# A mixture-of-experts layer pair: slots lent and freed by other rules, scatter ordered behind gate/up, a hint on a jump; and one attention layer without GpSimd arithmetic

## The chip, the cores and the metric

The kernel runs on one core of one Trainium2 chip. The core has five engines with instruction queues of their own: TensorE (PE, matrix products, with its weight loads shown as PEld), VectorE (DVE), ScalarE (ACT), GpSimd (POOL) and SyncE (SP, which here only issues transfers). Transfers between the chip's memory (HBM) and the on-chip memory (SBUF) run on 16 DMA engines. The metric is the time of one execution in microseconds (us), lower is better.

## The reference

Two stacks of two layers each run on 256 tokens of width 1024. The first stack has causal attention with rotary positions, a gated feed-forward layer, an RWKV layer and a second feed-forward layer. The second has differential attention, attention to a memory and a mixture of experts (MoE), then sparse latent attention, attention to the memory and a second MoE. The change touches the first attention layer and both MoE layers:

```python
def moba_attention(x, w_qkv, w_o, cos, sin):
    q, k, v = jnp.split(x @ w_qkv, 3, axis=-1)
    q = apply_rope(to_heads(q), cos, sin)       # 16 heads of 64
    k = apply_rope(to_heads(k), cos, sin)
    ...
    p = jax.nn.softmax(s_all, axis=-1)          # causal scores
    ...
    return out @ w_o

def hierarchical_moe(x, w_group, b_group, w_expert, b_expert, w_gate, w_up, w_down):
    ...
    top_w = jax.nn.softmax(top_val, axis=-1) * g_gate      # 2 of 16 experts for each token
    combine = jnp.sum(jax.nn.one_hot(expert_id, N_EXPERTS) * top_w[..., None], axis=1)
    y = jnp.zeros_like(t)
    for e in range(N_EXPERTS):
        hid = jax.nn.silu(t @ w_gate[e]) * (t @ w_up[e])   # width 512
        y = y + combine[:, e:e + 1] * (hid @ w_down[e])
    return y
```

Each MoE layer is followed by `layer_norm(alpha * h + moe(h))`. All is in float32, and 16 experts with three matrices of 2 MB each have to be read for each MoE layer.

## The kernel before

**The program.** One straight line of code; a scheduler puts each engine's instructions in an order, and each engine runs its own list strictly in that order. In the profile the first attention layer lies at 0 to 152 us, the first MoE layer's expert loop at 1048 to 1268 us, the second's at about 1466 to 1685 us.

**The MoE loop** (`moe`) takes the experts in eight pairs, q = 0 to 7. For each pair it

- multiplies the gathered tokens `xg` with the gate and then the up matrices (line 1669, 32 matmuls each; `gu`),
- forms `hid` = silu(gate) * up (line 1674 on ACT, line 1675 on DVE), turns it with four transposes (line 1684, tile `mm<-c_ident,hid`) and copies it to `hT` (line 1689, DVE),
- in the odd pairs below 7, gathers the tokens of the next two pairs (line 1632, 32 matmuls),
- multiplies `hT` with the down matrices (line 1711, 32 matmuls) and scales the result into the tiles `Y` (line 1716 ACT, line 1717 DVE),
- adds `Y` of the pair before to the layer's result in two halves, by matmuls with the selection `sT` (`scatter`, line 1655, tile `acc`). The second half is ordered behind the turn of `hid` (`issue_after(turned)`); the first half and `select_T` (lines 1642 and 1644, which make `sT` and the scales `cs`) carry no such order, so that the scheduler may put them anywhere.

**The weights** come through a ring (`MoeQueue`): 1 MB pieces in a fixed order, each into the slot at the head of a list of free slots. `take(4)` hands out four pieces, `done(4)` gives their slots back and issues as many transfers as there are free slots. Besides its own slots (`mw`) the ring borrows buffers that other parts of the layer need again at its end: `nrm`, `g`, `xh` and `h`. `h` is the residual of the layer, which in the meantime lives as two parts `hh` and `hl`. A borrowed slot gets no further piece when at most KK = 8 pieces are still to be loaded. Before the end of the layer `h` is built again (line 1698: `h = hh + hl`, two operations of DVE), and the buffer `g` gets the layer norm's factors by two transfers on ACT's queue (`gb<-in_ln_g_dram`, `gb<-in_ln_b_dram`).

**The jump.** A dense fallback (`moe_dense`) stands in the program between the last down matmuls of pair 7 (n == 6), under `tc.If(over > 64, ...)`. It isn't needed with this data: every engine jumps over it. After it come the rest of the down matmuls' work, `scatter(7, 1)`, the residual addition (`deep_add`, line 396) and the layer norm.

**The first attention layer** projects q and k of two heads at a time (`proj`, 48 matmuls of lines 225 to 227 for each step j, eight steps). Each weight piece is split into a high part `wh` (ACT, line 201) and a low part `wl = w - wh` (line 202), here on GpSimd for q and k (16 operations of 128x1024). The rotation multiplies with cos and sin on DVE (lines 466 and 470) and adds both on GpSimd (line 471, `qk`, 8 operations of 128x512). `moba_scores` then makes the scores (lines 491 and 492), masks, maxima and exponentials, and scales them (lines 500 to 511, DVE and ACT, tiles `st` and `s`); `moba_pv` turns them on PE (line 520) and multiplies with v (lines 525 and 526).

Of the kernel before, what the change touches and what calls it, by code (L numbers as in the profile page):

```python
# [15 lines left out]
ALU = mybir.AluOpType  # L16
# [39 lines left out]
class MoeQueue:  # L56
# [20 lines left out]
    def add(self, pool, n):  # L77
        self.free += [(pool, "mw", True, 1)] * n

    def once(self, pool, tag, parts=1):  # L80
        self.free.append((pool, tag, False, parts))

# [39 lines left out]

    def done(self, n):
        for slot in self.ring[self.used - n:self.used]:
            if slot[2] or len(self.queue) - len(self.loaded) > KK:
                self.free.append(slot)
        self.fetch()


class Block:  # L130
# [304 lines left out]
    def moba(self, h):  # L435
# [3 lines left out]
        with tc.tile_pool(name="at", bufs=2) as at, tc.tile_pool(name="at1", bufs=1) as at1:  # L439
# [13 lines left out]
            cb, sb = (a.unsqueeze(1).broadcast_to([128, 2, 256]) for a in (cos, sin))  # L453
            streams = [self.cols(wqkv[:, a * 1024:a * 1024 + 1024], nc.gpsimd) for a in range(2)]

            def proj(j):
                w = [f(j) for f in streams]
                p = self.acc()
                pv = p.rearrange("p (a n) -> p a n", a=2)
                for a in range(2):  # L460
                    for k in range(8):
                        self.mm3(pv[:, a], [y[:, k] for y in w[a]], [y[:, k] for y in x], k == 0, k == 7)
                m1 = at.tile([128, 2, 256], F32, name="m1")
                m2 = at.tile([128, 2, 256], F32, name="m2")
                qk = at.tile([128, 2, 256], F32, name="qk", bufs=3)
                nc.vector.tensor_tensor(m1, pv, cb, op=ALU.mult)
                for q in range(4):
                    a, b = 32 * q, 32 * (q ^ 1)
                    nc.scalar.copy(m2[b:b + 32], pv[a:a + 32])
                nc.vector.tensor_tensor(m2, m2, sb, op=ALU.mult)  # L470
                nc.gpsimd.tensor_tensor(qk, m1, m2, op=ALU.add)
                return qk
# [1123 lines left out]
    def moe(self, h, x32, r, li, last=False):  # L1596
# [5 lines left out]
        with ExitStack() as es:  # L1602
# [11 lines left out]
            mq.once(self.xp, "xh")  # L1614
            mq.once(self.hp, "h")
            mq.fetch()
# [45 lines left out]
            for q in range(8):  # L1662
                gu = []
                for m in range(2):
                    w = mq.take(4)
                    ps = self.ps()
                    for k in range(8):
                        for e in range(2):
                            mm(ps[64 * e:64 * e + 64], xg[:, k, q % 2 * 128 + e * 64:q % 2 * 128 + e * 64 + 64], mq.slab(w[2 * (k // 4) + e], k % 4),  # L1669
                               start=k == 0, stop=k == 7)  # L1670
                    mq.done(4)
                    gu.append(ps)
                hid = mo.tile([128, 512], F32, name="hid")
                act.activation(hid, gu[0], AF.Silu)
                tt(hid, hid, gu[1], op=ALU.mult)  # L1675
                if q == 0:
                    over = nc.values_load(r["cnti"][0:1, 0:1], min_val=0, max_val=512)
                if prev is not None:
                    scatter(q - 1, 0, *prev)
                old = prev  # L1680
                sT, cs = select_T(q, sel)
                p = self.ps()
# [7 lines left out]
                if q % 2 and q < 7:  # L1690
                    sel = select(q + 1)
                    xg = gather(sel)
                if q == 5:
                    h = self.hp.tile([128, 2, 1024], F32, tag="h", name="h")
# [7 lines left out]
                for n, (hf, k) in enumerate(order):  # L1702
                    if q == 7 and n == 6:
                        with tc.If(over > 64, preferred_fallthrough_block=False):
                            self.moe_dense(mo, h, li, r["Co"])
                    for e in range(2):
# [4 lines left out]
                        mm(pd[hf][64 * e:64 * e + 64], hT[:, k, 64 * e:64 * e + 64], b, start=k == 0, stop=k == 3)  # L1711
                mq.done(4)
                Y = []
# [337 lines left out]
```

## Time and profile before

| what | value |
|---|---|
| median of 3 runs | 1703.74 us (1700.69 to 1705.14) |
| the profiled execution | 1703.31 us |
| its span, first to last instruction | 1701.2 us, so 2.1 us lie around it |
| PE busy | 1588.7 us (93%) |
| DVE busy | 840.1 us (49%) |
| ACT busy | 655.8 us (39%) |
| POOL busy | 95.8 us (6%) |
| mean granted clock of TensorE | 0.971 of full speed |

Most of the span is matrix products, one after another; the time that is not is found by looking for idle stretches of PE and for what ended them. A row of the timeline gives the start, the duration, the engine, the line, the operation, the tiles written and read, and in brackets how long the engine stood idle before it and what released it. A row of the windows gives, for one stretch, how long each engine was busy in it, the clock granted to TensorE (1.00 is 2.4 GHz, 0.50 is 1.2 GHz), and the share and rate of the DMA engines.

### The profile page before, as it was taken

What the parts mean: (1) busy time and instruction counts of PE and PEld (TensorE: products, weight loads), DVE (VectorE), ACT (ScalarE), POOL (GpSimd) and SP (SyncE); (2) the same over time, 40 slices, a digit from 0 to 9 for tenths busy, and PEclk for the clock granted to TensorE, in tenths of its full rate; (3) what the DMA queues carried; (4) which work ended last, traced back from release to release, by engine and by line L of the source; (5) the groups of instructions that cost most, each with busy time, mean ns of one, the idle gap of its engine ahead of it and who ended that gap; (6) DMA issues with size and microseconds to landing.
All of it is one profiled execution on the core that took longest, in us unless ns stands there. A gap on an engine that the chain in (4) does not pass through costs nothing. (4 is left out here: it accounts for less than half of the span.)

```text
span 1701.2 us, 24789 instructions
## 1 busy us (share of the span) xinstructions
PE 1588.7 (93%) x9871; PEld 1157.7 (68%) x9871; DVE 840.1 (49%) x1831; ACT 655.8 (39%) x1228; POOL 95.8 (6%) x98
## 2 busy tenths in 40 slices
PE   7899999989999999999999798999878989899996
PEld 6777999968767669999788785443327778544342
DVE  3566666475666347665558644111227964511113
ACT  5675555322344236554467432101016744210111
POOL 3610000001100000000101000000000000000000
PEclk9999999989899999999999899999999999999998
DMA  9333755233223448552661846999949257699993
GB/s 345 128 118 115 232 176 173 59 100 112 88 76 104 125 160 263 196 175 98 235 235 42 336 182 230 416 415 416 375 174 327 95 215 284 239 416 414 416 393 125
DMA packets 169771, 375.31 MB, mean 221 GB/s; under 512 B 17188, under 2 KB 106028, under 8 KB 155052
## 3 DMA queue, kind: packets, MB, share of 16 engines
q1 hardware_dynamic: 159696, 363.40, 58.6%
q10 hardware_dynamic: 9948, 10.19, 1.9%
q8 instruction: 82, 1.34, 0.3%
q14 instruction: 45, 0.37, 0.1%
HBM read 372.52 MB, written 1.05 MB: 220 GB/s over the span
## 5 line engine op out<-in xcount | busy, mean ns | idle before, releaser
L202 DVE TENSOR_TENSOR wl<-w,wh 128x1024 fp32r<-128x1024 f32 (+1 forms) x205 | 245.9, 1208 | 178.4 <-ACT wh L201 177.9
L201 ACT CAST wh<-w 128x1024 fp32r<-128x1024 f32 (+1 forms) x221 | 226.8, 1038 | 209.9 <-PE mm L226 125.6
L1669 PE MATMUL mm<-mw,xg 128*64 128x512 f32 x1024 | 231.4, 594 | 0.0
L225 PE MATMUL mm<-xh,wh 128*128 128x256 f32 x800 | 227.2, 284 | 0.4 <-ACT wh L201 0.4
L227 PE MATMUL mm<-xh,wl 128*128 128x256 f32 x800 | 227.4, 284 | 0.0
L226 PE MATMUL mm<-xl,wh 128*128 128x256 f32 x800 | 227.2, 284 | 0.0
L1669 PEld LDWEIGHTS mm<-mw,xg 128*64 128x64 f32 x1024 | 77.6, 137 | 140.6 <-issue 139.8
L225 PEld LDWEIGHTS mm<-xh,wh 128*128 128x128 f32 x800 | 152.4, 190 | 2.5 <-ACT wh L201 0.7
L226 PEld LDWEIGHTS mm<-xl,wh 128*128 128x128 f32 x800 | 151.7, 190 | 2.0
L227 PEld LDWEIGHTS mm<-xh,wl 128*128 128x128 f32 x800 | 151.9, 190 | 0.0
L1711 PE MATMUL mm<-mw,hT 128*64 128x512 f32 x512 | 116.5, 599 | 2.2 <-issue 2.2
L225 PE MATMUL acc<-wh,xh 128*128 128x512 f32 x284 | 113.4, 405 | 1.8 <-ACT xh L263 1.2
L226 PE MATMUL acc<-wl,xh 128*128 128x512 f32 x284 | 114.2, 403 | 0.1
L227 PE MATMUL acc<-wh,xl 128*128 128x512 f32 x284 | 113.5, 401 | 0.0
L1716 ACT ACTIVATE Y<-mm,cs 128x512 fp32r<-128x512 f32 x32 | 22.0, 687 | 166.8 <-PE mm L1711 166.8
L1711 PEld LDWEIGHTS mm<-mw,hT 128*64 128x64 f32 x512 | 39.2, 138 | 69.0 <-issue 67.9
L1675 DVE TENSOR_TENSOR hid<-hid,mm 128x512 f32<-128x512 f32 x16 | 11.0, 688 | 147.2 <-PE mm L1669 147.2
L1717 DVE SCALAR_TENSOR_TENSOR Y<-mm,cs,Y 128x512 fp32r<-128x512 f32 x32 | 24.0, 751 | 117.7 <-ACT Y L1716 115.9
L227 PE MATMUL acc<-wh,fl 128*128 128x512 f32 x176 | 69.8, 396 | 0.0
L225 PE MATMUL acc<-wh,fh 128*128 128x512 f32 x176 | 69.5, 395 | 0.0
L226 PE MATMUL acc<-wl,fh 128*128 128x512 f32 x176 | 69.3, 394 | 0.0
L225 PEld LDWEIGHTS acc<-wh,xh 128*128 128x128 f32 x284 | 53.6, 189 | 14.9 <-ACT xh L263 1.6
(522 smaller groups left out, 2797.5 us busy)
## 6 DMA issues: line engine op xcount, KB each, us to landing
mw<-in_moe_w_down_dram SPq DMA_DIRECT2D x62, 1024.0 KB, 15.6
mw<-in_moe_w_gate_dram SPq DMA_DIRECT2D x58, 1024.0 KB, 8.8
mw<-in_moe_w_up_dram SPq DMA_DIRECT2D x56, 1024.0 KB, 19.9
w<-in_ffn_w_gate_dram SPq DMA_DIRECT2D x22, 1024.0 KB, 6.5
w<-in_ffn_w_up_dram SPq DMA_DIRECT2D x22, 1024.0 KB, 5.4
w<-in_ffn_w_down_dram SPq DMA_DIRECT2D x22, 1024.0 KB, 5.0
w<-in_attn_w_qkv_dram SPq DMA_DIRECT2D x12, 1024.0 KB, 16.2
w<-in_rwkv_w_rkv_dram SPq DMA_DIRECT2D x24, 512.0 KB, 3.7
```

The costliest lines, as they stand in the source:

```text
L201: nc.scalar.copy(r[0], raw)
L202: (lo_eng or nc.vector).tensor_tensor(r[1], raw, r[0], op=ALU.subtract)
L225: mm(out, lhs[0], rhs[0], start=start, stop=False)
L226: mm(out, lhs[0], rhs[1], start=False, stop=False)
L227: mm(out, lhs[1], rhs[0], start=False, stop=stop)
L1669: mm(ps[64 * e:64 * e + 64], xg[:, k, q % 2 * 128 + e * 64:q % 2 * 128 + e * 64 + 64], mq.slab(w[2 * (k // 4) + e], k % 4), start=k == 0, ...
L1675: tt(hid, hid, gu[1], op=ALU.mult)
L1711: mm(pd[hf][64 * e:64 * e + 64], hT[:, k, 64 * e:64 * e + 64], b, start=k == 0, stop=k == 3)
L1716: act.activation(y[0], pd[hf], AF.Copy, scale=cs)
L1717: vec.scalar_tensor_tensor(y[1], pd[hf], cs, y[0], op0=ALU.mult, op1=ALU.subtract)
```

## The change

It does six things. A slot now carries a number `keep`: it gets a new piece only when more than that many are still to be loaded. For `h` the number is 22 instead of 8, so that it gets no piece after one that is used in pair 4 (first MoE layer) or 5 (second); before, its last piece was used in pair 6 and 7. Slots are given back two at a time, halfway through each group of four, instead of four at its end. `scatter(q - 1, 0)` and `select_T` are ordered behind the last gate/up matmul (`issue_after(full)`). `h` is built again in pair 6 of the code instead of pair 5. The branch gets a label, the block becomes the one that is fallen into, and in pair 7, ahead of `hid`, a place is marked for a hint that the jump is likely taken. In the first attention layer the low weight parts of q and k and the sum of the rotation go from GpSimd to DVE.

```diff
@@ -75,10 +75,10 @@
                         self.queue.append((wd[e, c * 256:c * 256 + 256, :].rearrange("(k p) f -> p k f", p=128), 2))
 
     def add(self, pool, n):
-        self.free += [(pool, "mw", True, 1)] * n
-
-    def once(self, pool, tag, parts=1):
-        self.free.append((pool, tag, False, parts))
+        self.free += [(pool, "mw", 0, 1)] * n
+
+    def once(self, pool, tag, parts=1, keep=KK):
+        self.free.append((pool, tag, keep, parts))
 
     def fetch(self, n=99):
         while n and self.free and len(self.loaded) < len(self.queue):
@@ -120,9 +120,10 @@
             return w[k // n][:, k % n]
         return w[:, k]
 
-    def done(self, n):
-        for slot in self.ring[self.used - n:self.used]:
-            if slot[2] or len(self.queue) - len(self.loaded) > KK:
+    def done(self, n, later=0):
+        end = self.used - later
+        for slot in self.ring[end - n:end]:
+            if len(self.queue) - len(self.loaded) > slot[2]:
                 self.free.append(slot)
         self.fetch()
 
@@ -451,7 +452,7 @@
                     nc.scalar.copy(v[:, t, hf * 512:hf * 512 + 512], acc[t][hf])
             o = self.xT()
             cb, sb = (a.unsqueeze(1).broadcast_to([128, 2, 256]) for a in (cos, sin))
-            streams = [self.cols(wqkv[:, a * 1024:a * 1024 + 1024], nc.gpsimd) for a in range(2)]
+            streams = [self.cols(wqkv[:, a * 1024:a * 1024 + 1024]) for a in range(2)]
 
             def proj(j):
                 w = [f(j) for f in streams]
@@ -468,7 +469,7 @@
                     a, b = 32 * q, 32 * (q ^ 1)
                     nc.scalar.copy(m2[b:b + 32], pv[a:a + 32])
                 nc.vector.tensor_tensor(m2, m2, sb, op=ALU.mult)
-                nc.gpsimd.tensor_tensor(qk, m1, m2, op=ALU.add)
+                nc.vector.tensor_tensor(qk, m1, m2, op=ALU.add)
                 return qk
 
             qk, sm = {}, {}
@@ -1612,7 +1613,7 @@
             mq.once(self.gp, "nrm", 2)
             mq.once(self.gp, "g", 2)
             mq.once(self.xp, "xh")
-            mq.once(self.hp, "h")
+            mq.once(self.hp, "h", keep=22)
             mq.fetch()
 
             def select(q):
@@ -1666,19 +1667,23 @@
                     ps = self.ps()
                     for k in range(8):
                         for e in range(2):
-                            mm(ps[64 * e:64 * e + 64], xg[:, k, q % 2 * 128 + e * 64:q % 2 * 128 + e * 64 + 64], mq.slab(w[2 * (k // 4) + e], k % 4),
-                               start=k == 0, stop=k == 7)
-                    mq.done(4)
+                            full = mm(ps[64 * e:64 * e + 64], xg[:, k, q % 2 * 128 + e * 64:q % 2 * 128 + e * 64 + 64], mq.slab(w[2 * (k // 4) + e], k % 4),
+                                      start=k == 0, stop=k == 7).ins
+                        if k % 4 == 3:
+                            mq.done(2, 2 - k // 4 * 2)
                     gu.append(ps)
+                if q == 7:
+                    tc.mark_branch_hint_location("dense", hint="LikelyTaken")
                 hid = mo.tile([128, 512], F32, name="hid")
                 act.activation(hid, gu[0], AF.Silu)
                 tt(hid, hid, gu[1], op=ALU.mult)
                 if q == 0:
                     over = nc.values_load(r["cnti"][0:1, 0:1], min_val=0, max_val=512)
-                if prev is not None:
-                    scatter(q - 1, 0, *prev)
                 old = prev
-                sT, cs = select_T(q, sel)
+                with tc.issue_after(full):
+                    if prev is not None:
+                        scatter(q - 1, 0, *prev)
+                    sT, cs = select_T(q, sel)
                 p = self.ps()
                 for f in range(4):
                     turned = pe.transpose(p[:, f * 128:f * 128 + 128], hid[:, f * 128:f * 128 + 128], self.ident).ins
@@ -1690,7 +1695,7 @@
                 if q % 2 and q < 7:
                     sel = select(q + 1)
                     xg = gather(sel)
-                if q == 5:
+                if q == 6:
                     h = self.hp.tile([128, 2, 1024], F32, tag="h", name="h")
                     for t in range(2):
                         nat, *parts = (v[:, t].rearrange("p (c a b) -> p c a b", c=2, a=a) for v, a in
@@ -1701,7 +1706,7 @@
                 order = [(hf, k) for hf in range(2) for k in range(4)] if q == 7 else [(hf, k) for k in range(4) for hf in range(2)]
                 for n, (hf, k) in enumerate(order):
                     if q == 7 and n == 6:
-                        with tc.If(over > 64, preferred_fallthrough_block=False):
+                        with tc.If(over > 64, label="dense", preferred_fallthrough_block=True):
                             self.moe_dense(mo, h, li, r["Co"])
                     for e in range(2):
                         if q == 7:
@@ -1709,7 +1714,9 @@
                         else:
                             b = mq.slab(w[2 * (k // 2) + e], k % 2)[:, hf * 512:hf * 512 + 512]
                         mm(pd[hf][64 * e:64 * e + 64], hT[:, k, 64 * e:64 * e + 64], b, start=k == 0, stop=k == 3)
-                mq.done(4)
+                    if n == 3:
+                        mq.done(2, 2)
+                mq.done(2)
                 Y = []
                 for hf in range(2):
                     y = [mo.tile([128, 512], F32R, name="Y%d%d" % (hf, n)) for n in range(2)]
```

The lines of the changed kernel stand up to seven further down (1711 becomes 1716, 1669 becomes 1670, 1655 becomes 1656, 1684 becomes 1689). Where the instructions stand on three engines is shown in the following rows.

PE, first MoE layer, pair 5 before: the down matmuls of pair 4 (line 1711), then gate and up of pair 5 (line 1669) up to the turn of `hid` (line 1684).

```order
L1711 MATMUL mm<-mw,hT 64x512 x16
L1655 MATMUL acc<-Y_10521,sT 128x512 x2
L1655 MATMUL acc<-Y_10522,sT 128x512 x2
L1669 MATMUL mm<-mw,xg 64x512 x17
L1642 MATMUL mm<-c_ident,sel 128x128 x2
L1644 MATMUL mm<-C,sel 128x2 x2
L1669 MATMUL mm<-mw,xg 64x512 x15
L1684 MATMUL mm<-c_ident,hid 128x128 x4
```

The same place of the changed kernel (lines 1716, 1670 and 1689; the scatter is line 1656, `select_T` lines 1643 and 1645):

```order
L1716 MATMUL mm<-mw,hT 64x512 x16
L1670 MATMUL mm<-mw,xg 64x512 x32
L1656 MATMUL acc<-Y_10519,sT 128x512
L1656 MATMUL acc<-Y_10520,sT 128x512
L1656 MATMUL acc<-Y_10519,sT 128x512
L1656 MATMUL acc<-Y_10520,sT 128x512
L1643 MATMUL mm<-c_ident,sel 128x128 x2
L1645 MATMUL mm<-C,sel 128x2 x2
L1689 MATMUL mm<-c_ident,hid 128x128 x4
```

The scatter and the selection moved from inside the gate and up matmuls to between them and the turn. Before, this split stands in pairs 4 to 7 of the first layer and 5 to 7 of the second; in the other pairs the rows were like those of the changed kernel.

DVE, first MoE layer, before, from the `Y` tiles of pair 5 to the `hT` of pair 6:

```order
L1717 SCALAR_TENSOR_TENSOR Y_10677<-mm,cs,Y_10676 128x512
L1717 SCALAR_TENSOR_TENSOR Y_10681<-mm,cs,Y_10680 128x512
L1649 COPY cs<-mm 64x1 x2
L1698 TENSOR_TENSOR h<-hh,hl 128x2x4x128 x2
L1675 TENSOR_TENSOR hid<-hid,mm 128x512
L1689 COPY hT<-mm 128x512
```

The changed kernel, from the `Y` tiles of pair 4 to the `hT` of pair 5 (the two halves of `h` are line 1703):

```order
L1724 SCALAR_TENSOR_TENSOR Y_10520<-mm,cs,Y_10519 128x512
L1703 TENSOR_TENSOR h<-hh,hl 128x2x4x128
L1724 SCALAR_TENSOR_TENSOR Y_10524<-mm,cs,Y_10523 128x512
L1703 TENSOR_TENSOR h<-hh,hl 128x2x4x128
L1679 TENSOR_TENSOR hid<-hid,mm 128x512
```

The two operations moved one pair ahead, to between two `Y` tiles, where the next instruction is the `hid` of pair 5. In the second layer of the changed kernel they stand behind both `Y` tiles of pair 4 and directly ahead of that `hid`.

DVE, first attention layer, the changed kernel, one step from the maxima (`st`) of one pair of heads over the rotation of a later one to the scaling of the scores:

```order
L203 TENSOR_TENSOR wl<-w,wh 128x1024
L501 TENSOR_SCALAR st<-st 128x4
L467 TENSOR_TENSOR m_527<-acc,cos 128x512
L203 TENSOR_TENSOR wl<-w,wh 128x1024
L508 RECIPROCAL st<-st 128x4
L511 TENSOR_SCALAR s<-s,st 128x128
L512 TENSOR_SCALAR s<-s,st 128x256
L511 TENSOR_SCALAR s<-s,st 128x128
L512 TENSOR_SCALAR s<-s,st 128x256
L471 TENSOR_TENSOR m_528<-m_528,sin 128x512
L496 TENSOR_TENSOR s<-mm,msk 128x128
L472 TENSOR_TENSOR qk<-m_527,m_528 128x512
```

Before, the same stretch of DVE has neither the two `wl` rows nor the `qk` row. On PE, the changed kernel has 17 of the next step's projection matmuls between the scores of one pair of heads and the turn of the scaled scores of the pair before it; before, there were none to two there in most steps.

## Rows read from the trace of the kernel before

**Rows 1.** Windows, first MoE layer: stretch, length, busy (xcount), clock, DMA share, GB/s.

```profile
1089.90:1113.90 24.00, 23.90 (x115) 9.22 (x114) 3.88 (x7) 2.34 (x4) 0.00 (x0) 1.00 1.02 416
1113.90:1141.60 27.70, 27.62 (x146) 14.52 (x146) 4.56 (x9) 3.52 (x6) 0.00 (x0) 1.00 1.02 418
1141.60:1167.80 26.20, 25.42 (x116) 9.41 (x114) 3.88 (x7) 2.34 (x4) 0.00 (x0) 1.00 1.02 415
1167.80:1198.10 30.30, 29.47 (x147) 13.53 (x146) 4.56 (x9) 3.52 (x6) 0.00 (x0) 1.00 1.02 414
1198.10:1228.90 30.80, 26.13 (x116) 9.74 (x116) 7.67 (x9) 2.34 (x4) 0.00 (x0) 0.97 0.92 359
1228.90:1256.20 27.30, 26.46 (x117) 9.77 (x116) 3.19 (x6) 2.34 (x4) 0.00 (x0) 0.97 0.82 324
```

**Rows 2.** Windows, second MoE layer.

```profile
1591.40:1621.70 30.30, 29.41 (x146) 13.73 (x146) 4.56 (x9) 3.52 (x6) 0.00 (x0) 1.00 1.02 416
...
1647.80:1673.90 26.10, 25.32 (x115) 9.71 (x114) 7.01 (x8) 2.34 (x4) 0.00 (x0) 1.00 0.80 297
```

**Rows 3.** Timeline of PE, first MoE layer, pair 2, behind the up matmuls.

```profile
1110.63 1.20 PE L1655 MATMUL acc<-Y,sT 128*128 128x512 f32 x4
...
1112.25 0.63 PE L1684 MATMUL mm<-c_ident,hid 128*128 128x128 f32 x4
```

**Rows 4.** Timeline of PE, turns of hid, pairs 5 and 6, same layer.

```profile
1192.81 0.66 PE L1684 MATMUL mm<-c_ident,hid 128*128 128x128 f32 x4 [0.78 <-DVE hid L1675]
...
1226.61 0.64 PE L1684 MATMUL mm<-c_ident,hid 128*128 128x128 f32 x4 [4.67 <-DVE hid L1675]
```

**Rows 5.** Timeline of DVE ahead of hid, pair 6, same layer.

```profile
1221.97 3.79 DVE L1698 TENSOR_TENSOR h<-hh,hl 128x1024 f32<-128x1024 f32 x2 [6.28 <-PE mm L1669]
```

**Rows 6.** Waits of SP in both MoE layers: us, times, longest.

```profile
SPq L91 <- DMA gb<-in_ln_g_dram: 18.1, 1, 18.1
...
SPq L95 <- DMA gb<-in_ln_g_dram: 19.4, 1, 19.4
```

**Rows 7.** Timeline of DVE, first operation behind the jump, both MoE layers.

```profile
1270.84 0.69 DVE L396 SCALAR_TENSOR_TENSOR h<-h,acc 128x512 f32<-128x512 f32 x1 [3.50 <-issue]
...
1688.18 0.69 DVE L396 SCALAR_TENSOR_TENSOR h<-h,acc 128x512 f32<-128x512 f32 x1 [3.11 <-issue]
```

**Rows 8.** Timeline of PE, first attention layer, turns of the scaled scores.

```profile
59.46 0.30 PE L520 MATMUL mm<-c_ident,s 128*128 128x128 f32 x1 [3.62 <-DVE s L510]
...
73.19 0.30 PE L520 MATMUL mm<-c_ident,s 128*128 128x128 f32 x1 [2.37 <-DVE s L510]
```

**Rows 9.** Timeline of DVE and POOL, first attention layer.

```profile
55.05 1.83 DVE L500 TENSOR_SCALAR st<-st 128x4 f32<-128x4 f32 x1
...
70.63 2.41 DVE L510 TENSOR_SCALAR s<-s,st 128x128 f32<-128x128 f32 x1
...
70.62 2.34 POOL L202 TENSOR_TENSOR wl<-w,wh 128x1024 fp32r<-128x1024 f32 x1 [1.24 <-ACT wh L201]
```

**Rows 10.** Windows, first attention layer, four steps from rotation to rotation.

```profile
56.80:69.60 12.80, 10.14 (x64) 9.06 (x66) 4.57 (x17) 9.52 (x28) 6.21 (x4) 0.87 0.46 164
69.60:83.80 14.20, 11.79 (x78) 9.88 (x78) 8.54 (x24) 8.36 (x20) 6.01 (x3) 0.88 0.01 2
...
93.20:103.00 9.80, 9.07 (x68) 7.54 (x67) 6.49 (x19) 7.29 (x20) 1.27 (x1) 1.00 0.32 107
103.00:113.40 10.40, 9.47 (x72) 7.93 (x74) 7.87 (x17) 7.81 (x20) 1.27 (x1) 1.00 0.24 71
```

**Rows 11.** Groups by line, 30 to 140 us: busy, mean ns, idle before.

```profile
L202 DVE TENSOR_TENSOR wl<-w,wh 128x1024 fp32r<-128x1024 f32 x9 | 11.5, 1273 | 3.9 <-ACT wh L201 3.9
...
L470 DVE TENSOR_TENSOR m<-m,sin 128x512 f32<-128x512 f32 x8 | 6.4, 800 | 10.1 <-ACT m L469 10.1
...
L202 POOL TENSOR_TENSOR wl<-w,wh 128x1024 fp32r<-128x1024 f32 x15 | 35.7, 2394 | 14.6 <-ACT wh L201 14.5
L471 POOL TENSOR_TENSOR qk<-m,m 128x512 f32<-128x512 f32 x8 | 10.2, 1279 | 30.7 <-DVE m L470 29.0 <-DVE st L500 1.7
```

## The prediction

> **What bounds the kernel now.** First I read the windows of the two MoE layers, cut at the start of each pair's down matmuls, and compared pairs that do the same work. In the first layer pair 2 takes 24.00 us and pair 3, which also gathers, 27.70 us; TensorE is busy for all but 0.1 us of either [rows 1]. Pairs 4 to 7 do the same work in 26.20, 30.30, 30.80 and 27.30 us. The second layer repeats it: 30.30 us for pair 5, 26.10 us for pair 7 and for pair 6 too, whose row is not shown [rows 2]. So TensorE bounds the loop, and the late pairs lose 2 to 7 us each. Then I read the timeline for what they wait for. In pair 2, 1.62 us of scatter and selection stand between the up matmuls and the turn of hid, and the turn starts without a wait [rows 3]. In pair 5 nothing is left to stand there, and the turn waits for hid on VectorE [rows 4]. In pair 6 that wait is 4.67 us [rows 4], because VectorE runs the two additions of h, 3.79 us, ahead of hid; they had themselves waited 6.28 us for gate/up matmuls, which still read the slot lent by h [rows 5].
>
> The transfers come second. They run at 414 to 418 GB/s, share 1.02, through the pairs from 1089.90 to 1198.10; then the share falls to 0.92 and 0.82 [rows 1]. SyncE's queue waits once for 18.1 us and, in the second layer, 19.4 us, for the transfer into gb [rows 6], which is behind a gate/up slot being read.
>
> At the jump over the dense block VectorE stands 3.50 us and 3.11 us, released by nothing that the profile shows ("issue") [rows 7]. In the first attention layer TensorE waits 3.62 and 2.37 us for the scaled scores [rows 8]; ahead of each, a small VectorE operation lasted 1.83 and 2.41 us, the latter over the same time as a GpSimd wl of 2.34 us [rows 9]. The granted clock of these steps is 0.87 and 0.88, which mixes 1.2 GHz stretches behind the waits with 2.4 GHz [rows 10].
>
> **Scatter and selection behind the up matmuls, h one pair earlier.** The late pairs become like pairs 2 and 3: 24.0 us, or 27.7 us with a gather. First layer: 26.2 - 24.0 = 2.2, 30.3 - 27.7 = 2.6, 30.8 - 24.0 = 6.8 and 27.3 - 24.0 = 3.3, together 14.9 us [rows 1]. Part of the 6.8 and 3.3 is the clock, 0.97 in both rows against 1.00. Second layer: 2.6 + 2.1 + 2.1 = 6.8 us [rows 2]. The additions of h (3.79 us) are no longer late in pair 6. In the first layer they lie between two Y of pair 4, with the gate and up blocks of pair 5, 14 us, ahead of the hid behind them. In the second they precede the hid of pair 5 directly and their slot is read until half the up matmuls are done, so hid may come 0.3 us late: a pair of 24.0 us holds three blocks of 32 matmuls and, by estimate, 3 us of the rest, so a block takes 7 us, and 3.79 - 3.5 = 0.3. The 1.62 us of scatter and selection that now stand before the turn [rows 3] cover it; without them it would cost 0.3 us.
>
> **Can the weights follow?** After 1228.90 the first layer moves 27.3 us x 324 GB/s = 8.8 MB, which at 418 GB/s takes 21.2 us: landed at 1250.1, 6.1 us ahead of the last down matmuls at 1256.20. The DMA engines also stand idle (1 - 0.92/1.02) x 30.8 + (1 - 0.82/1.02) x 27.3 = 8.4 us [rows 1]. So the stream allows 6.1 us if none of the idle time goes, 14.5 us if all does. The idle time follows the wait for gb [rows 6], and gb waits for matmuls of pair 6, which come earlier themselves; the last half of the weights is also used half a block, 3.5 us, after 1256.20. I take 13 of the 14.9, ends 6.1 and 14.9. In the second layer gb follows the gate of pair 7, so pairs 5 and 6 pull it in by 4.7 us; ends 4.7 and 6.8, and I take 6.8, since the second half is again needed only later.
>
> **Slots by number and by halves.** The slot of h takes its last piece earlier, so that the others must carry one more piece late; the transfers' order on SyncE stays as it was, and so does what each waits for. A piece can follow only when the last matmul that read the slot is done, which giving it back earlier in the code doesn't change. I cost it at nothing; what hides the smaller ring is the lead of 6.1 us above, and without it a piece of 1 MB at 418 GB/s costs 2.5 us.
>
> **The jump.** It is taken in both versions; the hint ahead of it is new. No row shows a hinted jump. The ends are 0 and 3.50 + 3.11 = 6.6 us [rows 7]; all engines pass, and what follows is a chain to the layer's end. I take 5, three quarters, nearer to the full wait since the marked place lies pair 7's down matmuls ahead of the jump. The hint's own instructions I cost at nothing, hidden behind those matmuls. The Trainium skill ("Runtime: NRT & Kernel Launch", section "Instruction fetch mechanics") says that fetching ahead is purely sequential and that a taken jump out of the fetched window waits for the target's fetch. The trace agrees for the jump without a hint (3.50 us); by that rule alone the term is 0, and the sum comes 5 us later. What a hint does, the page doesn't say.
>
> **First attention layer.** GpSimd loses 16 wl of 2.39 us and 8 sums of 1.28 us; VectorE gains 16 x 1.27 = 20.4 us and, by the rotation's second product, also 128x512, 8 x 0.80 = 6.4 us, 26.8 us in all [rows 11]. The two late steps 93.20 to 113.40 already ran nearly so: no wl on GpSimd, one to three on VectorE, VectorE busy 6.49 and 7.87 us, clock 1.00, 9.80 and 10.40 us long [rows 10]. Taking their mean of 10.1 for the two stalled steps gives 12.80 + 14.20 - 20.2 = 6.8 us; I take 7. Upper end: four steps at TensorE's busy 9.07 us give 47.2 - 36.3 = 10.9 us. Lower end: all of VectorE's 26.8 us on the path against the 6.8 won, 20 us lost. The 17 projection matmuls that now stand ahead of the turn of the scores give VectorE time, so I stay near the late steps.
>
> **Sum.** 13 + 6.8 + 0 + 5 + 7 = 31.8 us. The profiled execution took 1703.31 us, 0.4 us under the median of the three runs: 1703.3 - 31.8 = **1671.5 us**.
>
> **Rivals.**
> - *The jump waits as before.* For it: nothing before shows a hint at work, and the jump is still taken. Against: the marked place gives time to fetch. 31.8 - 5 = 26.8, 1676.5 us. By the page's rule above it would be this one.
> - *VectorE replaces GpSimd as the late one in attention.* In the changed order the wl stand among the scores' operations, ahead of the reciprocal; if that costs as much as the two stalls, the 7 us vanish: 1678.5 us. Against: VectorE is busy 7.87 of 10.40 us in the fullest late step [rows 10].
> - *The weights bound the MoE layers.* 6.1 and 4.7 us instead of 13 and 6.8: 1703.3 - 22.8 = 1680.5 us. For it: the share of 1.02 over most of the loop [rows 1].
> - *Slower.* TensorE waits for VectorE in every step of the attention layer and the clock falls behind each wait as in the two stalled steps. VectorE's 26.8 us are 3.4 us a step; the clock's part is about 12% of a step of 13 us, 1.6 us [rows 10]. 8 x 5.0 = 40 us against 24.8 us won elsewhere: 1703.3 + 15 = 1718 us. It decides from 30 us, 3.7 us a step.
> - *The halves and numbers starve pair 7*, one piece of 2.5 us a layer: inside the first one's range.
>
> **How the numbers follow.** The forecast has 0.60 (1666 to 1676 by itself), the jump 0.16, VectorE in place of GpSimd 0.12, the weights 0.09, slower 0.03. Differences under 0.3%, 5.1 us, can't be told from no change here. 8 in 10 lie from 1664 (10.9 in attention, 6.6 at the jump, 14.9 in the first MoE layer would give 1664) to 1682 (the weights' case and some of VectorE's). The first four are faster; I leave 0.02 to no change, where half of VectorE's work lies on the path, and 0.03 to slower.
>
> **What would show it.** In both MoE layers' windows pairs 4 to 7 take 24.0 or 27.7 us, the turn of hid waits less than 1 us in pair 6, and the additions of h stand early. If a pair is longer with TensorE waiting for a transfer, the weights' case is right. Behind the jump VectorE's idle time falls from 3.5 to under 1 us; if it stays, the rival is right. In the attention layer no VectorE operation on 4 or 128 columns lasts over 1 us, and the steps take about 10 us at clock 1.00. The prediction is wrong if VectorE's wl are what TensorE waits for there, or if the stretches between the parts of the change move as well.

## The result, and the profile after

The changed kernel takes 1680.11 us (median of four runs, 1678.06 to 1682.98) against 1704.44 us for the kernel before on the same chip. The ratio is 0.986 with a 95% interval of 0.9836 to 0.9884: faster by 24.3 us. The forecast was 1671.5 us, range 1664 to 1682: direction and range hold, the middle is 8.6 us too low. The profiled execution took 1678.06 us.

The page's first lines:

```profile
span 1676.3 us, 24750 instructions
PE 1574.7 (94%) x9871; PEld 1160.8 (69%) x9871; DVE 857.3 (51%) x1855; ACT 656.4 (39%) x1228; POOL 47.7 (3%) x74
```

GpSimd's busy time fell from 95.8 to 47.7 us. VectorE's rose by 17.2 us, less than the 26.8 us counted: the operations that it had before became shorter in the attention layer, the scaling of 128x128 from a mean of 434 to 284 ns, those on four columns (line 500, now 501) from 414 to 158 ns, the second product of the rotation from 800 to 692 ns.

The windows of the first MoE layer, pairs 2, 4, 5, 6 and 7, columns as in [rows 1]:

```profile
1078.67:1102.77 24.10, 23.91 (x116) 9.27 (x115) 3.89 (x7) 2.35 (x4) 0.00 (x0) 1.00 1.02 415
1130.43:1154.53 24.10, 23.92 (x116) 9.28 (x115) 3.88 (x7) 2.35 (x4) 0.00 (x0) 1.00 1.02 414
1154.53:1182.20 27.67, 27.67 (x146) 15.29 (x146) 8.32 (x11) 3.52 (x6) 0.00 (x0) 1.00 1.02 414
1182.20:1206.30 24.10, 23.92 (x115) 9.27 (x115) 3.88 (x7) 2.34 (x4) 0.00 (x0) 1.00 1.02 413
1206.30:1233.43 27.13, 25.19 (x114) 10.92 (x115) 3.19 (x6) 2.34 (x4) 0.00 (x0) 1.00 1.00 396
```

and of the second, pairs 5 to 7:

```profile
1572.80:1600.50 27.70, 27.67 (x146) 15.36 (x146) 8.32 (x11) 3.52 (x6) 0.00 (x0) 1.00 1.02 416
1600.50:1624.60 24.10, 23.92 (x115) 9.27 (x115) 3.88 (x7) 2.34 (x4) 0.00 (x0) 1.00 1.02 414
1624.60:1648.72 24.12, 23.94 (x114) 11.43 (x115) 3.19 (x6) 2.34 (x4) 0.00 (x0) 1.00 0.99 386
```

Pairs 4 to 6 of the first layer and 5 to 7 of the second now last as long as the early ones, and the DMA share stays at 0.99 to 1.02 to the end. Only pair 7 of the first layer doesn't follow. The timelines of PE in pair 6 (first row) and pair 7 show why:

```profile
1204.57 0.63 PE L1689 MATMUL mm<-c_ident,hid 128*128 128x128 f32 x4
...
1221.49 3.65 PE L1670 MATMUL mm<-mw,xg 128*64 128x512 f32 x16 [0.42 <-DMA mw<-in_moe_w_up_dram]
1226.50 3.65 PE L1670 MATMUL mm<-mw,xg 128*64 128x512 f32 x14 [1.35 <-DMA mw<-in_moe_w_up_dram]
```

The turn of pair 6, which waited 4.67 us for VectorE [rows 4], waits no longer; in pair 7 the up matmuls now wait for their weights. The view of waits from 1206 to 1233 us has the same two waits at the weight loads (PEld), where they are longer:

```profile
PEld mm L1670 <- DMA mw<-in_moe_w_up_dram: 3.5, 2, 2.2
```

SyncE's wait for the transfer into gb fell from 18.1 and 19.4 us [rows 6] to 14.9 and 15.0:

```profile
SPq L91 <- DMA gb<-in_ln_g_dram: 14.9, 1, 14.9
...
SPq L95 <- DMA gb<-in_ln_g_dram: 15.0, 1, 15.0
```

The timeline of DVE behind the jump, both layers, answers to [rows 7]; the source view of the jump's line (duration shortest/median/longest in ns, first and last start) shows the branches themselves:

```profile
1248.64 0.69 DVE L397 SCALAR_TENSOR_TENSOR h<-h,acc 128x512 f32<-128x512 f32 x1 [4.07 <-PEq L1709]
...
1663.50 0.69 DVE L397 SCALAR_TENSOR_TENSOR h<-h,acc 128x512 f32<-128x512 f32 x1 [3.62 <-PEq L1709]
```

```profile
L1709 DVEq COMPARE_BRANCH  x2: 72/72/72, 1244.9 to 1659.9; - x2
L1709 PEldq COMPARE_BRANCH  x2: 3364/3450/3536, 1245.0 to 1660.0; - x2
...
L1709 DVEq EVENT_SEMAPHORE  x2: 21/21/21, 1247.9 to 1662.7; - x2
```

The wait is 4.07 and 3.62 us, no shorter than before, not under 1. TensorE stays 3.4 to 3.5 us inside its branch; VectorE's branch lasts 72 ns, but its next instruction starts 3.0 and 2.8 us later. TensorE's wait is not new. The source view of the kernel before, where each engine has two branches at the jump, a short one and the one that it waits at, has it too:

```profile
L1704 PEldq COMPARE_BRANCH  x4: 81/1699/3667, 1267.7 to 1685.5; - x4
```

The long ones are 3.67 and 3.30 us. Before, VectorE went on by itself, at 1270.84 us in the first layer, and waited 0.45 us for TensorE's products after two additions; in the changed kernel it waits for TensorE ahead of the first. So the first addition comes 0.5 us later, but the third stands where it did, 16.4 us behind the start of pair 7's down matmuls in both kernels (15.7 and 16.0 us in the second layer).

In the first attention layer, the turns of the scores that answer to [rows 8] and the two steps that answer to the first two of [rows 10]:

```profile
58.62 0.30 PE L521 MATMUL mm<-c_ident,s 128*128 128x128 f32 x1 [0.52 <-DVE s L511]
...
68.80 0.33 PE L521 MATMUL mm<-c_ident,s 128*128 128x128 f32 x1 [0.25 <-DVE s L511]
```

```profile
55.94:65.97 10.03, 9.22 (x70) 7.84 (x70) 7.68 (x23) 7.48 (x20) 0.00 (x0) 1.00 0.59 211
65.97:76.30 10.33, 9.69 (x74) 7.96 (x70) 7.67 (x21) 7.75 (x20) 0.00 (x0) 1.00 0.00 0
```

The two steps of 12.80 and 14.20 us are 10.03 and 10.33 us long, at a granted clock of 1.00 instead of 0.87 and 0.88.

**Where the time came from.** The start of the same instruction in both traces, before minus after, gives the sum so far. First instruction behind the attention layer (the turn of nrm): 151.28 - 144.75 = 6.5 us. Pair 2 of the first MoE: 11.2. The addition behind the first jump: 22.2. Pair 5 of the second MoE: 18.6. The addition behind the second jump: 24.7. The MoE loops gained 11.6 us (193.96 to 182.41 us from pair 0's down matmuls to pair 7's) and 6.6 us (186.00 to 179.41). The 4.7 us between attention and the MoE lie where the change has no instruction, mostly at 940 to 1050 us, where the granted clock was 0.92 before and 0.97 after. They are not counted as the change's: in the profiled executions of the other kernels with the whole attention edit and a changed MoE loop the lead at the first MoE loop is 3.2 (e8) to 10.3 us (e1) instead of 11.2. Of the 3.6 us lost between the MoE layers 2 are taken up below; the rest lies in stretches that the change doesn't touch.

### The profile page after: what moved, and what is told of

Read it like the earlier page. It is cut to its first block, busy times and chain, and to the rows that moved or that the text cites. A ratio compares the mean times of both kernels' runs of the same rounds, so it can differ in the third digit from the quotient of the medians.

```text
span 1676.3 us, 24750 instructions
## 1 busy us (share of the span) xinstructions
PE 1574.7 (94%) x9871; PEld 1160.8 (69%) x9871; DVE 857.3 (51%) x1855; ACT 656.4 (39%) x1228; POOL 47.7 (3%) x74
## 5 line engine op out<-in xcount | busy, mean ns | idle before, releaser
L203 DVE TENSOR_TENSOR wl<-w,wh 128x1024 fp32r<-128x1024 f32 (+1 forms) x221 | 265.1, 1207 | 188.9 <-ACT wh L202 188.2
L1670 PE MATMUL mm<-mw,xg 128*64 128x512 f32 x1024 | 224.1, 592 | 1.8 <-DMA mw<-in_moe_w_up_dram 1.8
L1670 PEld LDWEIGHTS mm<-mw,xg 128*64 128x64 f32 x1024 | 83.0, 137 | 138.8 <-issue 134.3
```

The source lines that it names most:

```text
L203: (lo_eng or nc.vector).tensor_tensor(r[1], raw, r[0], op=ALU.subtract)
L1670: full = mm(ps[64 * e:64 * e + 64], xg[:, k, q % 2 * 128 + e * 64:q % 2 * 128 + e * 64 + 64], mq.slab(w[2 * (k // 4) + e], k % 4), start=k ...
```

## Experiments: the parts of the change one by one

**e2, attention alone.** The kernel before with these two lines:

```diff
-            streams = [self.cols(wqkv[:, a * 1024:a * 1024 + 1024], nc.gpsimd) for a in range(2)]
+            streams = [self.cols(wqkv[:, a * 1024:a * 1024 + 1024]) for a in range(2)]
-                nc.gpsimd.tensor_tensor(qk, m1, m2, op=ALU.add)
+                nc.vector.tensor_tensor(qk, m1, m2, op=ALU.add)
```

> The kernel before with the edit of the first attention layer alone (low weight parts and the rotation's sum on VectorE). Theory: the two long waits of TensorE at 59.46 and 73.19 us go, TensorE is 7 us earlier behind the layer, and the time falls by about 7 us, give or take 2 us of clock later on. Rival (VectorE becomes the late one): the steps stay above 12 us and the gain is 0 to 2 us.

1698.02 us, ratio 0.9959 (0.9942 to 0.9976); 6.6 us ahead behind the layer, turns waiting 0.52 and 0.26 us. The attention edit alone gives all that the change gives in this layer.

**e3, scatter and selection behind the up matmuls alone.** The kernel before with

```diff
-                if prev is not None:
-                    scatter(q - 1, 0, *prev)
-                sT, cs = select_T(q, sel)
+                with tc.issue_after(full):
+                    if prev is not None:
+                        scatter(q - 1, 0, *prev)
+                    sT, cs = select_T(q, sel)
```

> The kernel before with the scatter and selection ordered behind the last up matmul alone; h is built and lent as before. Theory: pairs 4, 5 and 7 of the first layer and 5 to 7 of the second take 24.0 or 27.7 us; pair 6 of the first still waits for the two additions of h, some 3 us (4.67 less the 1.62 us that now stand before the turn) and loses clock after it. Gain 9 us in the first layer and 7 us in the second, 16 us in all. Rival (the weights bound the late pairs): TensorE waits for transfers in their place and the gain is under 8 us.

1690.43 us, 0.9909 (0.9883 to 0.9935). The loops gain 11.1 and 6.6 us, nearly as much as the whole change (11.6 and 6.6). Pair 6 lasts 26.84 us, since its turn still waits for VectorE, and pair 7 24.79 us. PE's timeline, pair 6:

```profile
1218.57 0.63 PE L1685 MATMUL mm<-c_ident,hid 128*128 128x128 f32 x4 [2.84 <-DVE hid L1675]
```

**e4, the h buffer alone**: `keep=22` for its slot and `h` built at `q == 6`, nothing else of the change.

> The kernel before with the slot of h lent for fewer pieces (22 instead of 8) and h built one pair later in the code, alone. Theory: in pair 6 of the first layer the wait for hid falls from 4.67 to 0.8 us and the half-clock stretch behind it goes: 5.6 us less in the first layer, nothing in the second. Rival (the smaller ring starves pair 7): TensorE waits for weights there and the gain is 0 to 3 us.

1701.25 us, 0.9977 (0.9965 to 0.999). The first loop gains 5.5 us and the second loses 0.5; the turn of pair 6 waits 0.78 us. e3 and e4 gain 16.6 us apart in the first loop and 11.6 together: with both, pairs 4 to 6 are as fast as the early ones, and pair 7 waits for its weights. The edit of h adds only 0.4 us to that of the scatter.

**e8, the changed kernel without the halves**: `done(4)` behind each group of four.

> The changed kernel with slots given back four at a time, as before. Theory (giving back by halves changes neither the order of the transfers nor what each waits for): pairs take 24.1 and 27.7 us, pair 7 of the first layer 27.1 us, the span stays within 2 us of 1676 us. Rival (the halves let transfers start earlier): pairs 4 to 7 get longer by some us.

One run, 1684.91 us; loops of 181.90 and 179.40 us against 182.41 and 179.41. Giving slots back by halves changes nothing in the loops. The longer time arose ahead of the MoE: the lead over the kernel before at the first loop is 3.2 us here and 11.2 in the change.

**e11, attention's sum on VectorE, but wl on GpSimd as before** (the first pair of lines of e2 not made).

> The changed kernel with the low weight parts of q and k back on GpSimd, only the rotation's sum on VectorE. Theory (GpSimd's low parts hold up the small operations of VectorE): the waits of TensorE at about 59 and 73 us are back, and TensorE is 4 to 7 us later behind the first attention layer than in the changed kernel. Rival (the order of the scores' turns behind 17 projection matmuls is what helped): at most 2 us later.

One run, 1690.14 us; behind the layer it is 4.3 us ahead, where the full edit is 6.5. The expectation of 4 to 7 us less failed: wl on VectorE is worth 2.2 us, and the sum with the order that came with it 4.3 us. One of the two stalls is gone (0.33 us), the other is half as long:

```profile
57.93 0.30 PE L521 MATMUL mm<-c_ident,s 128*128 128x128 f32 x1 [1.84 <-DVE s L511]
```

This step takes 12.3 us where the full edit has 10.0, which is the whole of the 2.2 us. The VectorE operation on 4 columns ahead of it, 1.83 us before [rows 9], takes 0.59 us here, which is 1.24 of the 1.78 us by which the wait fell. A scaling of 128x128 still takes long, as in [rows 9], over the same time as a GpSimd `wl`:

```profile
54.77 0.59 DVE L501 TENSOR_SCALAR st<-st 128x4 f32<-128x4 f32 x1
...
68.81 2.43 DVE L511 TENSOR_SCALAR s<-s,st 128x128 f32<-128x128 f32 x1
```

It costs nothing there: it is the second scaling of its step, and the turn at 68.69 us waited for the first. Before, the long one was the first (70.63 + 2.41 = 73.04 us), and the turn at 73.19 us waited for it.

## Experiments: pair 7 and its weights

**e5, the slot of h as before** (no `keep=22`), and `h` built in pair 7 behind `hT`, so that hid doesn't wait for it. If the smaller ring were the cause, pair 7 would be whole.

> The changed kernel, but the slot of h is lent as before (8 instead of 22) and h is built behind the hT of pair 7, where VectorE stands idle for the whole block of down matmuls. Theory (in the first MoE layer the ring is one slot short, so that pair 7 waits for up weights): pair 7 takes 24.1 to 25 us instead of 27.13 us, 2 to 3 us less in all; the second layer stays at 24.1 us for pairs 6 and 7. Rival (the wait of pair 7 comes from the transfers into gb alone, whatever the ring): 27.1 us again.

1682.33 us, 0.9858 (0.9825 to 0.989). Pair 7 takes 26.98 us and still waits for the up weights (1.6 us in two waits). The ring's lost slot is not the cause. What is left is the rate of the transfers. The windows of the whole first loop, before and after, from pair 0's down matmuls to pair 7's:

```profile
1062.23:1256.19 193.96, 186.65 (x895) 80.75 (x895) 32.30 (x56) 19.93 (x34) 0.00 (x0) 0.99 0.98 394
1051.02:1233.43 182.41, 179.91 (x894) 83.03 (x895) 32.28 (x56) 19.94 (x34) 0.00 (x0) 1.00 1.02 412
```

182.41 us at 412 GB/s are 75.2 MB, which at the 415 GB/s of the early pairs would take 181 us, by estimate. The change is within 2 us of that, and so are e1, e3, e5 to e9 and e11, with loops of 181.9 to 182.9 us, whether pair 6 or pair 7 is the long one.

**e10, the slot of g given up earlier too**, so that gb's transfer would not hold up SyncE's queue.

```diff
-            mq.once(self.gp, "g", 2)
+            mq.once(self.gp, "g", 2, keep=22)
```

> The changed kernel with the slot of g, too, lent only while more than 22 pieces are to be loaded. The two transfers into gb then come a pair or two earlier, and the weights behind them in SyncE's queue do not wait for a slot read in pair 6. Theory (pair 7 of the first MoE layer waits 3 us for weights because of SyncE's wait of 14.9 us for gb): pair 7 takes 24.1 to 25 us, 2 to 3 us less in all. Rival (the rate of the transfers bounds the layer, so that a slot less costs what the wait gave): pair 7 stays at 27 us or gets longer.

1691.85 us, 0.9924 (0.9903 to 0.9946), slower than the change. Pairs 6 and 7 take 26.70 and 30.39 us, pair 7 of the second layer 29.01 us. The theory was wrong, and the edit did not remove what it was aimed at: SyncE's queue still waits 19.4 and 19.6 us for gb, only earlier (from 1144 to 1164 us in the first layer). The windows around that wait and behind it:

```profile
1150.00:1170.00 20.00, 19.82 (x98) 9.01 (x95) 6.30 (x8) 1.75 (x3) 0.00 (x0) 1.00 0.78 297
1190.00:1238.00 48.00, 41.87 (x190) 15.62 (x188) 4.70 (x8) 4.32 (x7) 0.00 (x0) 1.00 1.02 414
```

In 20 us at 297 instead of 414 GB/s some 5.7 us of transfers are lost, by estimate. The loop is 5.9 us longer than the change's, and TensorE stands waiting for weights in pairs 6 and 7 while the transfers run at 414 GB/s. So what the stream loses early the late pairs pay in full, which shows its rate as the limit of this loop. What fewer slots cost and what the earlier wait cost was not separated.

## Experiments: the jump

In the trace of the changed kernel no engine has a hint instruction; the marked place left none. The trace of e1 has one for each of three engines and each layer (`BRANCH_PREFETCH_HINT`).

**e1, a real hint**, on each engine by name behind its last instruction of the kind in pair 7:

```diff
-                if q == 7:
-                    tc.mark_branch_hint_location("dense", hint="LikelyTaken")
+                if q == 7:
+                    for eng, at in ((mybir.EngineType.PE, full), (mybir.EngineType.Activation, silu), (mybir.EngineType.DVE, prod)):
+                        with tc.issue_after(at):
+                            tc.mark_branch_hint_location("dense%d" % li, hint="LikelyTaken", engines=[eng])
```

> This is the changed kernel with hints that exist as instructions: one each on TensorE, ScalarE and VectorE, in pair 7 directly behind the last up matmul, the silu and the product, and with a label of its own for each layer. The changed kernel's lists of instructions hold no hint at all. Theory (the hint was never issued, and a jump's wait is a fetch that a hint can start early): VectorE's idle time behind the jump falls from 4.07 and 3.62 us to under 1 us, the span from 1676.3 to about 1670 us. Rival (a hint does nothing for this jump): the idle times stay at 3.6 to 4.1 us and the time at 1680 us.

1679.13 us, 0.9852 (0.9831 to 0.9874): not told apart from the change. The source view of the jump and DVE's timeline:

```profile
L1711 DVEq COMPARE_BRANCH  x2: 78/84/90, 1246.1 to 1657.8; - x2
L1711 PEldq COMPARE_BRANCH  x2: 366/398/430, 1246.2 to 1657.8; - x2
...
L1711 DVEq EVENT_SEMAPHORE  x2: 21/21/21, 1249.0 to 1660.6; - x2
```

```profile
1249.22 0.69 DVE L397 SCALAR_TENSOR_TENSOR h<-h,acc 128x512 f32<-128x512 f32 x1 [3.45 <-DVEq L1711]
```

Half of the theory holds: TensorE's branch falls from 3.45 to 0.40 us. But VectorE's next instruction still starts 2.9 and 2.8 us after its branch, with its hint. The addition comes 0.6 us earlier in each layer than in the changed kernel (waits of 3.45 and 3.07 us), which is all that freeing TensorE wins.

**e7, VectorE's hint one pair earlier.**

> The kernel with real hints, but VectorE's hint stands one pair earlier, behind the product of pair 6. Theory (VectorE's hint in pair 7 was issued but its fetch did not hold): if distance in time was what it lacked, VectorE's idle time behind the jump falls from 3.45 and 3.07 us to under 1 us. Rival (a hint does not help VectorE's jump here at any distance): it stays at 3.0 to 3.5 us.

One run, 1677.96 us. VectorE's next instruction still comes 3.2 and 2.8 us after its branch: one pair more of distance is not what the hint lacked.

**e6, a short block**: `for e in range(4)` in `moe_dense`, so that the jump passes about a quarter of the instructions on each engine.

> The changed kernel with a fallback block of 4 experts instead of 16, so that the block that is jumped over is a quarter as long on each engine; the block isn't entered with this data, so nothing that runs is left out, but the fallback would be incomplete. Theory (the wait behind the jump is a fetch of the target, and it depends on how far the target lies: ScalarE, whose block is the shortest, has no such wait): VectorE's idle time behind the jump, 4.07 and 3.62 us, falls to about 1 us or under, and TensorE's branch of 3.45 us gets shorter or stays with no effect on VectorE; 5 to 6 us less in all. Rival (the wait is a fixed cost of a taken jump): 3 us and more remain.

1683.25 us, 0.987 (0.9843 to 0.9897). Now it is the other way round:

```profile
L1709 DVEq COMPARE_BRANCH  x2: 72/72/72, 1248.0 to 1665.0; - x2
L1709 PEldq COMPARE_BRANCH  x2: 3344/3440/3536, 1248.1 to 1665.1; - x2
L1709 DVEq EVENT_SEMAPHORE  x2: 21/21/21, 1248.6 to 1665.5; - x2
```

VectorE goes on after 0.6 us, TensorE's branch still takes 3.44 us, and the addition waits 4.07 and 3.62 us, exactly as in the changed kernel. Each engine has a wait of its own of about 3 us; taking away VectorE's wins nothing, taking away TensorE's 0.6 us a layer (e1).

**e9, the whole fallback in two blocks of half the size**, one for each 128 tokens, with hints for both jumps. It does all the work of the fallback.

> The changed kernel with a complete fallback in two blocks, one for each half of the tokens, so that each jump of VectorE passes 96 instructions instead of 190, and with real hints for both jumps on TensorE, ScalarE and VectorE in pair 7. Theory (TensorE's branch needs a hint, 3.45 to 0.40 us; VectorE's wait needs a short jump, as with the block of 4 experts; either alone buys nothing because the other one waits): VectorE's idle time behind the jumps falls to 1 to 1.5 us and the time falls by 5 to 6 us to about 1674 us. Rival (the second jump on TensorE is not covered by its hint, or 96 instructions are still too far for VectorE): 3 us and more remain and the time stays at 1680 us.

1683.33 us, 0.9874 (0.9854 to 0.9893). At the first jump both waits are gone; the second has TensorE's again:

```profile
1247.95 0.69 DVE L397 SCALAR_TENSOR_TENSOR h<-h,acc 128x512 f32<-128x512 f32 x1 [1.11 <-DVEq L1713]
...
1252.97 0.69 DVE L397 SCALAR_TENSOR_TENSOR h<-h,acc 128x512 f32<-128x512 f32 x1 [4.32 <-PEq L1713]
```

TensorE's first branch took 0.42 us, its second 4.91 us: of two hints given in a row, only that of the first jump served. VectorE went on 0.6 us after either branch.

**e12, the jump ahead of pair 7's down matmuls** (`n == 0`), with a hint for TensorE behind the last gate matmul.

> The changed kernel with the fallback block moved ahead of pair 7's first down matmul (n == 0 instead of 6), and one real hint, on TensorE, behind the last gate matmul of pair 7. The block stays complete. Theory (TensorE's jump needs a hint, and VectorE's fetch of 3 us costs nothing where VectorE has nothing to do: behind hT it stands idle for about 5 us): no idle time of 3 us and more is left behind the down matmuls, VectorE's first residual addition starts within 1.5 us of the last Y, TensorE's branch takes 0.4 us; 6 us less in all, about 1674 us where the changed kernel gives 1680 us. Rival (the wait only moves, to TensorE at the start of the down matmuls): TensorE stands 3 us there and the time stays at 1680 us.

1682.15 us, 0.9853 (0.9829 to 0.9877). TensorE no longer waits behind the down matmuls, but at their start, for VectorE's jump:

```profile
1241.96 7.28 PE L1719 MATMUL mm<-mw,hT 128*64 128x512 f32 x18 [4.08 <-DVEq L1712]
```

The wait only moved. In the first layer the granted clock behind it is 0.50, 1.2 GHz, for 5.6 us of the down matmuls; in the second it stays at 1.00.

## Why the prediction was right in direction and 8.6 us off

**Attention: 7 forecast, 6.5 measured.** The late steps were the right pattern: the VectorE operations on 128 and 4 columns take 284 ns (line 511, 16 of them) and 158 ns (line 501, 8), and the steps take 10 us at clock 1.00. The two stalled steps gave 27.0 - 20.4 = 6.6 us, where 6.8 were worked out; the step ahead of them gained another 1.0 us and the two behind lost 1.4, from 9.5 and 9.8 to 10.3 us, so that part of the agreement is luck. That the long small operations cause the stalls holds for the second stall, by the times of the scaling and of the turn, and for part of the first: 1.84 us of it stand in e11 without a long operation. Of the 4.3 us that e11 wins, what comes from the sum's engine and what from the order with more projection matmuls ahead of the turn was not separated.

**First MoE: 13 forecast, 11.6 measured.** All late pairs became as short as the early ones but pair 7, as "can the weights follow?" had it possible: it waits for up weights (0.42 and 1.35 us at the matmuls, 3.5 at the weight loads) and is 3.0 us longer than 24.1. e5 shows that the ring's lost slot isn't the reason, and e10 and the windows of the loop that the rate of the transfers is the limit. The rival "the weights bound the MoE layers" had the right limit and the wrong place for it, 6.1 us: the transfers lost less time than before, 412 instead of 394 GB/s, as the prediction had argued.

**Second MoE: 6.8 forecast, 6.6 measured. Slots by number and halves: 0 forecast, 0 measured** (e8, e5).

**The jump: 5 forecast, 0 measured.** This is the step that failed, as written: "the hint ahead of it is new", and three quarters of 6.6 us for it. There is no hint in the changed kernel's instructions. And a real one would not have won the 5 us either (e1): it takes away TensorE's wait alone, for 0.6 us a layer, while VectorE has a second wait of nearly equal length beside it. The row with one releaser, "issue" [rows 7], did not show that there were two; the source view of the branch, 3.67 and 3.30 us on TensorE in the kernel before, would have. The rival "the jump waits as before" (1676.5 us, 0.16) had the mechanism. That the weights' rival, 1680.5 us, lies nearest to the measured time is luck: the loops gained 11.6 and 6.6 us, not its 6.1 and 4.7. The time lies outside the 1666 to 1676 us that the forecast gave to its own case; what held is the range that took in the rivals. By the Trainium skill ("Runtime: NRT & Kernel Launch", section "Instruction fetch mechanics") a taken jump out of the fetched window waits for its target. The 3.4 to 3.5 us of TensorE's branch and e6, where VectorE's wait goes when the target is near, agree with that; where the window ends no run shows.

**The stretch behind the first layer norm: not forecast, about 2 us lost.** The prediction named "if the stretches between the parts of the change move as well" as what would make it wrong. The windows of before (first two rows) and after (last two), the same work:

```profile
1278.70:1290.00 11.30, 11.09 (x54) 9.23 (x55) 9.58 (x14) 6.32 (x11) 0.92 (x1) 0.87 0.67 208
1290.00:1304.60 14.60, 12.29 (x64) 9.91 (x62) 8.22 (x41) 8.57 (x21) 1.40 (x2) 1.00 1.06 353
```

```profile
1256.00:1268.00 12.00, 11.96 (x55) 10.34 (x56) 9.64 (x14) 6.82 (x11) 0.92 (x1) 0.78 0.63 184
1268.00:1283.90 15.90, 13.58 (x63) 10.88 (x62) 9.82 (x47) 8.32 (x21) 1.41 (x2) 0.89 1.06 346
```

The granted clock is at half, 1.2 GHz, for longer than before: 25.9 us became 27.9. The other kernels with a changed MoE loop show 0.88 to 0.90 in the second part and lost 1.3 to 2.2 us there, all but e9, the one with two jumps, whose second part is like before:

```profile
1271.00:1285.60 14.60, 12.29 (x64) 9.89 (x62) 8.23 (x41) 8.55 (x21) 1.40 (x2) 1.00 1.04 349
```

e2, with the old loop, shows 1.00 too and lost nothing. So the faster loop alone doesn't decide it, since e9 has that; what TensorE does around the jump differs in e9, but which part of it decides was not tried.

**The sum.** 6.5 + 11.6 + 6.6 + 0 + 0 = 24.7 us, less 2 for the last stretch: 22.7 us. Between the two traces the span fell by 24.9 us, and that the terms come so near is in part luck: the 4.7 us won ahead of the MoE and the 3.6 us lost between its layers nearly cancel. The measured 24.3 us differ from the sum by less than the spread of one kernel's runs (up to 3 us from the median, mean granted clock 0.969 to 0.974).

## What to carry to other kernels

Compare stages that do the same work at different times of a loop: the shortest is a price list for the others. It gave 14.9 and 6.8 us here, and 11.6 and 6.6 were measured, since the weights could not follow all of the first. A feature that a line of code asks for, as a branch hint, is counted only when its instruction stands in the engine's list. A stall that ends on two engines at once is worth little until both are freed, so each engine's own instructions at the place are read before a price is put on it. Two edits that each shorten the same loop don't add up once the next limit, here the weights' rate, is reached.

## What was not expected of the hardware

- The taken jump costs TensorE 3.4 to 3.5 us inside the branch itself (3.3 to 4.1 over all runs without a hint), and 0.40 us with a hint given behind the last up matmul of the pair (e1). ScalarE's branch takes 0.05 us, and its next instruction comes 0.1 to 0.4 us later.
- VectorE's branch takes 0.07 us, but the next instruction comes 2.8 to 3.0 us later (up to 3.5 us in e12) where the whole block is passed (190 instructions, as e9's expectation counts them), and 0.6 us later for a quarter of the experts (e6) or at either of two half blocks with hints (e9). A hint on VectorE, one pair ahead or in the same pair, changed nothing for the whole block (e1, e7). Why is open.
- Of two hints in a row on TensorE the second jump's had no effect: 4.91 and 4.56 us in the two layers (e9).
- A 128x128 scaling on VectorE of 284 ns lasts 2.43 us beside a GpSimd `wl` of 2.57 us (e11) and was yet no stall there, since no turn waited for it.
